# A two-layer hybrid decoder on one core: the final norm goes into the loop over halves of the last tiles, and the hooked parts get new places

## The chip, the cores and the metric

One core of a Trainium2 chip runs the whole program in one launch. The metric is device time in microseconds (us), as the median of several runs; the profile shows one execution of the program. Times in this document are counted from the start of the profiled span.

## The reference

The input x is 512 tokens of 1024 numbers, mem is 256 tokens of 1024, all in 32-bit floats. Two layers follow each other, then a final RMS norm:

```
for l in range(DEPTH):
    xn = rmsnorm(h, norm_mix_g[l])
    c_q, c_kv, k_r, u = split(xn @ w_in[l])
    a_out = mla_group(c_q, c_kv, k_r, ...)        # causal attention, 8 heads, low-rank q and kv, rope
    s_out = s5_group(u, lam, log_dt, b, c, d, w_glu, b_glu)   # 32 groups, 64 complex states, scan, gelu, gate
    h = h + concat(rmsnorm(a_out, ga), rmsnorm(s_out, gs)) @ w_out[l]
    h = h + memory_cross_attention(rmsnorm(h, gx), rmsnorm(mem, gm), w_xq, w_xkv, w_xo)
    h = h + (silu(rmsnorm(h, gf) @ w_gate[l]) * (rmsnorm(h, gf) @ w_up[l])) @ w_down[l]
return rmsnorm(h, final_norm_g)
```

rmsnorm(x, g) is x / sqrt(mean(x^2) + 1e-6) * g over the 1024 (or 512) numbers of a token.

## The kernel before, in words

Everything is held transposed: h is eight tiles (hs[0] to hs[7]) of 128 features by 512 tokens. Each weight block is loaded into a tile wraw and split into a high part whi (ScalarE, ACT, L213) and a low part wlo (VectorE, DVE, L214), and activations likewise into hi and lo (with the gain of a norm: ghi and glo, L245 and L246). A product is then three matmuls of TensorE (PE): high by high, low by high, high by low (mm3, L220 to L222). mm, f, s and t are PSUM tiles; s5b, tmp, tmps, P are buffers in SBUF that several steps share; raw holds matrices that are read from HBM as they are.

A norm (rms) squares and sums the tiles (ACT L264, DVE L267), sums over features with matmuls against ones (L298), makes the statistic on DVE (L301), its power of -1/2 on GpSimd (POOL, L303), and spreads it to a row R over all partitions: ACT makes the high part (L280), DVE the low part (L281), PE multiplies both with the identity (L285), ACT copies the result to R (L306).

Within a layer the order of the code is: input projection (u, c_kv, k_r, c_q), memory norm (memg, its splits are at L245 and L246), the latent attention in units u of one head and query block each, the mix norm of both groups' outputs and w_out (L996 to L998, L1010 to L1012), cross attention, feed-forward. The state-space group and the cross attention's keys and values are cut into parts that are called at units of the attention by the table PLAN: p are steps of the state-space parameters (L374 to L573), v the s-matmuls on u (L820), c the two halves of the scan (L838 to L847, L867), m and y the output (L882, L885), G the gelu (L902), g the gate (the matmuls into t, L918, L919), x the cross attention's keys and values (xv: L961 to L963), s the state-space half of the mix norm. FPLAN does the same for layer 1's parameter steps at tiles of layer 0's feed-forward. The scheduler issues what is ready by a running priority; OFFS, P_OFF, PR_UP and MS_UP shift that priority for a part, so that a part can be issued earlier or later than where it is called. A simulated timeline decides the final order on each engine.

MST_POOL, POOLQ and IN_POOL choose what POOL does in DVE's place: the memory's square sums (L394, seven of 128x256), a share of layer 1's parameter products (L573, L509; twelve of 128x512), the low parts of some input-projection weights (L214).

The last feed-forward chunk of layer 1 leaves its last two output tiles (TAIL = 2) for the end and computes them by halves of 256 tokens. final() then squares and scales the tiles, makes the norm of each half and multiplies the eight tiles of the half by R (L1149): half 1 all on DVE, half 2 with tiles 2 and 6 on POOL. Two tiles go out with each store on the DMA queue of SyncE (SP).

Of the kernel before, what the change touches and what calls it, by code (L numbers as in the profile page):

```python
# [13 lines left out]
AF = mybir.ActivationFunctionType  # L14
ALU = mybir.AluOpType
# [10 lines left out]
EPS = 1e-6  # L26
# [3 lines left out]
KT = DM // 128  # L30
# [18 lines left out]
HALVES = (slice(0, 256), slice(256, 512))  # L49
# [89 lines left out]
class Trunk:  # L139
    def __init__(self, ctx, tc, A, out, depth=L, dbg=None):  # L140
        self.tc, self.nc, self.A, self.out, self.dbg = tc, tc.nc, A, out, dbg or {}
        self.sb = ctx.enter_context(tc.tile_pool(name="sb", bufs=1))
        self.ps = ctx.enter_context(tc.tile_pool(name="ps", bufs=1, space=PSUM))
        self.dr = ctx.enter_context(tc.tile_pool(name="dr", bufs=1, space=DRAM))
        self.depth = depth
        self.stop = self.STOP or depth
        self.n = self.np = 0
# [3 lines left out]


    XKV_POOL = ()
    GLU_POOL, MG_POOL, QK_POOL, ROPE_POOL, MST_POOL = 1, 0, 0, 0, 1
    POOLQ = ((), (1, 3))
    P_OFF = (500, 3000)
    SQ_PARTS, XLO_POOL = (0, 2, 4), ()
    IN_POOL = ((2, 5), (3, 6))
    KE_POOL, GL_POOL = ((0, 2), (0, 2)), ((), ())
    MN_POOL, MW_POOL = ((), ()), ((), ())  # L160
    YT, GT = "f", "t"
# [3 lines left out]


    PLAN = ((
# [5 lines left out]
    ), (  # L173
# [4 lines left out]
    ))  # L178
    OFFS = ({"x": 150, "m": 400, "s": 200, "c": 150, "G": 100, "v": 700, "g": 100, "y": -250, "p": 100},
            {"y": -700, "c": 250, "v": 50, "g": 800, "m": 850, "G": 1300, "p": 100, "x": -100, "s": -50})  # L180
    FPLAN = (0, 0, 1, 1, 1, 1, 1, 1, 2, 5)
    PR_UP, MS_UP = 1500, 2300

    def t(self, shape, tag, dtype=F32, name=None):
        self.n += 1
# [100 lines left out]
                                 start=x is hi, stop=x is lo)  # L286
        return ps

    def rms(self, acc, dim):

        nc = self.nc
        acc = acc if isinstance(acc, list) else [acc]
        n = acc[0].shape[-1]
        nb = n // 128
        ps = self.p("t")
        for b in range(nb):
            for i, x in enumerate(acc):
                nc.tensor.matmul(ps[:, b:b + 1], x[:, b * 128:(b + 1) * 128], self.ones, start=i == 0,  # L298
                                 stop=i == len(acc) - 1)
        ms = self.t([128, 4], "stat")[:, :nb]  # L300
        nc.vector.tensor_scalar(ms, ps[:, :nb], 1.0 / dim, EPS, ALU.mult, ALU.add)  # L301
        col = self.t([128, 4], "stat")[:, :nb]
        nc.gpsimd.tensor_tensor(col, ms, self.mhalf[:, :nb], ALU.pow)  # L303
        ps2 = self.row(col)
        R = self.t([128, 512], "R")[:, :n]
        nc.scalar.activation(R, ps2, AF.Copy)  # L306
        return col, R


# [107 lines left out]
    def s5_gen(self, l):  # L417
# [86 lines left out]
        def cmul_wide(wk, ri, t0, x, y, op, qs):  # L504
            E = V if ri == 0 or (qs.start // 4) not in self.POOLQ[l] else P
            tt = self.t([128, 4, 8, 16], "tmps")
# [5 lines left out]
        for q in range(4):  # L512
# [14 lines left out]
        for q in range(4):  # L527
# [569 lines left out]
    def ffn(self, l, hook):  # L1097
        nc, A = self.nc, self.A
        if l + 1 < self.depth:
            self.dh = self.dram([KT, 128, S], f"dh{l}")  # L1100
        X, R = self.normed(l, "ffn")
        for ci, (k0, nk) in enumerate(FF_CHUNKS):
            Ys = []
            for m in range(k0, k0 + nk):
                pg = self.pm()
                self.mm_block(A["w_gate"][l, m], X, pg)
                gf = self.t([128, 512], "tmp")
                nc.vector.tensor_tensor(gf, pg, R, ALU.mult)  # L1108
                nc.scalar.activation(gf, gf, AF.Silu)
                pu = self.pm()  # L1110
                self.mm_block(A["w_up"][l, m], X, pu)
                uf = self.t([128, 512], "tmp")
                nc.vector.tensor_tensor(uf, pu, R, ALU.mult)  # L1113
                nc.gpsimd.tensor_tensor(uf, uf, gf, ALU.mult)  # L1114
                Ys.append(self.split(uf))
                hook(m)
            last = ci == len(FF_CHUNKS) - 1
            nt = self.TAIL if last and l + 1 == self.depth else 0
            for m in range(KT - nt):
                ps = self.pm()  # L1120
                self.mm_block(A[f"w_down{ci}"][l, m], Ys, ps)
                self.residual(ps, m, self.dh if last and l + 1 < self.depth else None)
                hook(22 + 8 * ci + m)
            if nt:
                ws = [self.load_w_slots(A[f"w_down{ci}"][l, m]) for m in range(KT - nt, KT)]
                for cs in HALVES:
                    for m in range(KT - nt, KT):
                        ps = self.pm()[:, :256]
                        self.mm3(ps, [([w[:, k % 4 * 128:k % 4 * 128 + 128] for w in ws[m - KT + nt][k // 4]],
                                       [y[:, cs] for y in Ys[k]]) for k in range(nk)])  # L1130
                        h = self.hs[m][:, cs]
                        nc.vector.tensor_tensor(h, ps, h, ALU.add)

    def final(self):
        nc = self.nc
        hs = self.hs
        acc = None
        n0 = KT - self.TAIL
        for k in range(n0):
            acc = self.square(acc, hs[k])  # L1140
            nc.scalar.activation(hs[k], hs[k], AF.Copy, scale=self.fin[:, k:k + 1])
        for cs in HALVES:
            for k in range(n0, KT):
                self.square(acc[:, cs], hs[k][:, cs])
                nc.scalar.activation(hs[k][:, cs], hs[k][:, cs], AF.Copy, scale=self.fin[:, k:k + 1])
            _, R = self.rms(acc[:, cs], DM)
            for k in range(KT):
                h = hs[k][:, cs]
                (nc.gpsimd if cs.start and k % 4 == 2 else nc.vector).tensor_tensor(h, h, R, ALU.mult)  # L1149
                if k % 2 == 1:  # L1150
                    nc.sync.dma_start(self.out[k - 1:k + 1, :, cs].rearrange("k p t -> p k t"),
                                      self.hb[k // 4][:, k % 4 - 1:k % 4 + 1, cs])

    def part(self, f, i, off):
        with self.later(off):
# [2 lines left out]
    def run(self):  # L1158
        with self.later(-3 * self.PR_UP):
            self.setup()  # L1160
        for l in range(self.stop):
            self.l = l
            with (self.later(-2 * self.PR_UP) if l == 0 else nullcontext()):
                X, R, du = self.in_proj(l)
            if l == 0:
# [4 lines left out]
                for u, f, i in self.PLAN[0]:  # L1170
                    if u == -4:
                        self.part(params, i, self.OFFS[0].get("p", 0))
            with (self.later(-self.PR_UP) if l == 0 else nullcontext()):
                self.load_u(du)
                if l == 0:
                    for u, f, i in self.PLAN[0]:
                        if u == -3:
                            self.part(params, i, self.OFFS[0].get("p", 0))
                self.in_proj2(l, X, R)
# [5 lines left out]
            for u, f, i in self.PLAN[l]:  # L1185
                if u < -2:
                    continue
                hooks.setdefault(u, []).append((self.part, (parts[f], i, self.OFFS[l].get(f, 0))))
            for f, a in hooks.get(-2, ()):
# [8 lines left out]
            def hook(u):  # L1198
                for i, x in enumerate(self.FPLAN if params else ()):
                    if x == u:  # L1200
                        self.part(params, i, 0)
            self.ffn(l, hook)
        self.final()


@with_exitstack
# [16 lines left out]
```

## Time and profile before

| what | value |
|---|---|
| median of three runs | 1598.01 us (1595.21 to 1603.22) |
| the profiled execution | 1595.71 us |
| its span | 1593.9 us |
| mean granted clock of PE | 0.97 |
| PE busy | 1519.3 us, 95% |
| DVE, ACT, POOL busy | 908.6, 627.0, 169.7 us |
| DMA | 173 MB, mean 109 GB/s |

The span is the time from the first to the last event of the profiled execution. PE's clock is given as a share of 2.4 GHz; 1.2 GHz is 0.50. A timeline row gives the start, the busy time, the engine, the line, the operation, what it writes and reads, and how often it stands there in a row; in brackets how long the engine was idle before and what ended that. The waits list sums such idle times by what ended them. The windows add up each engine's busy time in a stretch.

### The profile page before, as it was taken

How to read it: one execution, taken by the hardware profiler on the slowest of the kernel's cores; microseconds unless marked ns; L12 is line 12 of the kernel's file. 1: busy time of each engine (PE TensorE's matmuls, PEld its weight loads, DVE VectorE, ACT ScalarE, POOL GpSimd, SP SyncE). 2: the span in 40 equal slices, each digit the busy share in tenths (PEclk: the TensorE clock that was granted, in tenths of full speed). 3: DMA queues.
4: the chain of work that ended last, by engine and by line, in shares of the span. 5: the costliest groups of instructions: out<-in, count | busy, mean ns of one | idle time of the engine just before them, and what ended most of it. 6: DMA issues, size and time to landing. Idle time of an engine off the chain costs nothing.

```text
span 1593.9 us, 20203 instructions
## 1 busy us (share of the span) xinstructions
PE 1519.3 (95%) x8038; PEld 1258.6 (79%) x8038; DVE 908.6 (57%) x1274; ACT 627.0 (39%) x1027; POOL 169.7 (11%) x123
## 2 busy tenths in 40 slices
PE   7977999999999999999999899999999999999997
PEld 6766877887877888888886788778887888888886
DVE  7997546657685535435444954465655443543554
ACT  5543475444342322223333456644434222222333
POOL 4300001111131101101100100101000100110110
PEclk9987998999999999999999899999999999999998
DMA  6646633211352332232338454422122223223231
GB/s 222 156 139 152 131 121 119 94 67 53 126 146 93 112 106 93 87 112 93 109 132 158 127 143 124 138 74 93 40 79 94 79 93 106 93 87 112 93 92 62
DMA packets 93278, 173.27 MB, mean 109 GB/s; under 512 B 16512, under 2 KB 49792, under 8 KB 93184
## 3 DMA queue, kind: packets, MB, share of 16 engines
q1 hardware_dynamic: 93184, 171.99, 36.3%
q8 instruction: 63, 1.03, 0.3%
q14 instruction: 31, 0.25, 0.1%
HBM read 152.10 MB, written 17.76 MB: 107 GB/s over the span
## 4 chain that ended last, share of the span: by engine, by line
PE 83%; DVE 6%; DMA 4%; ACT 4%; issue 1%; SPq 1%; POOL 0%; DVEq 0%; ACTq 0%; POOLq 0%
PE mm L220 14%; PE mm L222 13%; PE mm L221 13%; PE f L220 7%; PE f L222 7%; PE f L221 7%; PE mm L768 2%; DVE lo L243 1%; PE t L760 1%; DVE wlo L214 1%; DMA s5b<-dQ 1%; ACT whi L213 1%; PE f L961 1%; PE f L962 1%; PE f L963 1%
## 5 line engine op out<-in xcount | busy, mean ns | idle before, releaser
L213 ACT ACTIVATE whi<-wraw 128x1024 fp32r<-128x1024 f32 (+1 forms) x234 | 243.6, 1043 | 643.8 <-PE mm L221 290.4
L214 DVE TENSOR_TENSOR wlo<-wraw,whi 128x1024 fp32r<-128x1024 f32 (+1 forms) x227 | 312.6, 1378 | 99.0 <-ACT whi L213 96.5
L220 PE MATMUL mm<-hi,whi 128*128 128x512 f32 x580 | 227.3, 392 | 0.5 <-ACT whi L213 0.5
L221 PE MATMUL mm<-lo,whi 128*128 128x512 f32 x580 | 225.8, 390 | 0.0
L222 PE MATMUL mm<-hi,wlo 128*128 128x512 f32 x580 | 225.7, 390 | 0.0
L220 PE MATMUL mm<-ghi,whi 128*128 128x512 f32 (+1 forms) x352 | 138.3, 393 | 1.6 <-DVE tmp L1108 0.8
L222 PE MATMUL mm<-ghi,wlo 128*128 128x512 f32 (+1 forms) x352 | 138.7, 394 | 0.0
L221 PE MATMUL mm<-glo,whi 128*128 128x512 f32 (+1 forms) x352 | 137.8, 391 | 0.2 <-DVE glo L243 0.2
L220 PEld LDWEIGHTS mm<-hi,whi 128*128 128x128 f32 x580 | 109.0, 188 | 26.0 <-ACT whi L213 2.8
L222 PEld LDWEIGHTS mm<-hi,wlo 128*128 128x128 f32 x580 | 108.8, 188 | 23.3 <-DVE wlo L214 0.4
L221 PEld LDWEIGHTS mm<-lo,whi 128*128 128x128 f32 x580 | 108.9, 188 | 22.4
L1114 POOL TENSOR_TENSOR tmp<-tmp,tmp 128x512 f32<-128x512 f32 x44 | 62.2, 1413 | 567.2 <-DVE tmp L1113 520.1
L220 PE MATMUL f<-ghi,whi 128*128 128x512 f32 (+1 forms) x304 | 107.0, 352 | 8.1 <-DVE s5b L950 2.4
L220 PE MATMUL f<-hi,whi 128*128 128x512 f32 x286 | 112.7, 394 | 1.6 <-DVE glo L243 1.4
L222 PE MATMUL f<-hi,wlo 128*128 128x512 f32 x286 | 111.9, 391 | 0.4 <-DVE wlo L214 0.4
L221 PE MATMUL f<-lo,whi 128*128 128x512 f32 x286 | 111.8, 391 | 0.0
L221 PE MATMUL f<-glo,whi 128*128 128x512 f32 (+1 forms) x304 | 106.6, 351 | 0.2 <-DVE glo L243 0.2
L222 PE MATMUL f<-ghi,wlo 128*128 128x512 f32 (+1 forms) x304 | 106.5, 350 | 0.3 <-DVE wlo L214 0.3
L969 DVE TENSOR_TENSOR s5b<-mm,s5b 128x512 f32<-128x512 f32 x53 | 36.6, 691 | 115.9 <-PE mm L222 96.7
L242 ACT ACTIVATE hi<-tmp 128x512 fp32r<-128x512 f32 (+1 forms) x100 | 62.5, 629 | 91.7 <-POOL tmp L1114 63.8
L220 PEld LDWEIGHTS mm<-ghi,whi 128*128 128x128 f32 (+1 forms) x352 | 66.0, 187 | 16.5 <-DVE tmp L1108 1.0
L222 PEld LDWEIGHTS mm<-ghi,wlo 128*128 128x128 f32 (+1 forms) x352 | 66.1, 188 | 14.8 <-DVE tmp L1108 0.3
(330 smaller groups left out, 2821.8 us busy)
## 6 DMA issues: line engine op xcount, KB each, us to landing
wraw<-w_gate SPq DMA_DIRECT2D x44, 512.0 KB, 3.3
wraw<-w_up SPq DMA_DIRECT2D x44, 512.0 KB, 3.3
wraw<-w_down SPq DMA_DIRECT2D x30, 448.0 KB, 3.3
wraw<-w_xkv SPq DMA_DIRECT2D x16, 512.0 KB, 4.0
wraw<-w_xv SPq DMA_DIRECT2D x16, 512.0 KB, 3.5
wraw<-w_out SPq DMA_DIRECT2D x16, 512.0 KB, 3.3
wraw<-w_xq SPq DMA_DIRECT2D x16, 512.0 KB, 3.3
wraw<-w_xo SPq DMA_DIRECT2D x16, 512.0 KB, 3.3
```

The source lines that it names most:

```text
L213: nc.scalar.activation(hi, raw, AF.Copy)
L214: (eng or nc.vector).tensor_tensor(lo, raw, hi.bitcast(F32), ALU.subtract)
L220: self.nc.tensor.matmul(ps, wh, xh, start=i == 0, stop=False)
L221: self.nc.tensor.matmul(ps, wh, xl, start=False, stop=False)
L222: last = self.nc.tensor.matmul(ps, wl, xh, start=False, stop=i == n - 1)
L242: a = nc.scalar.activation(hi, src, AF.Copy)
L243: b = eng.tensor_tensor(lo, src, hi.bitcast(F32), ALU.subtract)
L760: nc.tensor.transpose(pt[:, x * 128:(x + 1) * 128], p[ii][:, kb * 128:(kb + 1) * 128], self.ident)
L768: nc.tensor.matmul(po[64 * x:64 * x + 64, cs], vs[kb][:, (2 * pair + x) * 64:(2 * pair + x + 1) * 64], PT[x][:, kk * 256:min(n, kk * 256 + ...
L961: nc.tensor.matmul(o, xh[:, ts], wh[:, ks], start=hf == tb == k == 0, stop=False)
L969: self.nc.vector.tensor_tensor(self.hs[m], ps, self.hs[m], ALU.add)
L1114: nc.gpsimd.tensor_tensor(uf, uf, gf, ALU.mult)
```

## The change

The final norm is no longer a function behind the feed-forward but three that the loop over halves calls: tail_start squares and scales the six finished tiles, tail_end does the rest for each half as soon as its two tiles are done, tail_scale multiplies by the row. The row is made by two matmuls of plain 32-bit floats from POOL's power (L1163), with no split. Half 1's eight products are ordered behind half 2's statistic. Half 2's products read the row from PSUM on DVE (five) and from its copy on POOL (tiles 2, 4, 6).

PLAN, OFFS, P_OFF, FPLAN, PR_UP and MS_UP get new numbers, and the work that MST_POOL, POOLQ and IN_POOL gave to POOL goes to DVE (seven square sums, twelve parameter products; one low part of 128x512 in layer 0, two of 128x1024 in layer 1). R_UP = 0 shifts nothing, and PSB gives the PSUM tiles as many buffers as before. In the changed file the lines behind the table are 3 and more higher: L220 is L223, L285 is L288, L298 is L301, L820 is L829, L961 is L970.

```diff
-    GLU_POOL, MG_POOL, QK_POOL, ROPE_POOL, MST_POOL = 1, 0, 0, 0, 1
-    POOLQ = ((), (1, 3))
-    P_OFF = (500, 3000)
+    GLU_POOL, MG_POOL, QK_POOL, ROPE_POOL, MST_POOL = 1, 0, 0, 0, 0
+    POOLQ = ((), ())
+    P_OFF = (2850, 4550)
-    IN_POOL = ((2, 5), (3, 6))
+    IN_POOL = ((1, 3), ())
-        (2, "m", 1), (2, "x", 3), (3, "m", 2), (3, "m", 3), (3, "x", 4), (4, "c", 0), (4, "c", 1), (8, "y", 0),
-        (10, "y", 1), (11, "y", 2), (11, "y", 3), (13, "G", 0), (13, "g", 0), (14, "x", 5), (14, "g", 1),
-        (14, "x", 6), (14, "g", 2), (15, "g", 3), (16, "x", 7), (16, "s", 0),
+        (2, "m", 1), (2, "x", 3), (2, "m", 2), (3, "m", 3), (3, "c", 0), (3, "x", 4), (4, "c", 1), (5, "y", 0),
+        (9, "y", 1), (10, "y", 2), (10, "y", 3), (13, "G", 0), (13, "g", 0), (14, "g", 1), (14, "g", 2),
+        (15, "x", 5), (15, "x", 6), (15, "g", 3), (15, "x", 7), (16, "s", 0),
...
-    OFFS = ({"x": 150, "m": 400, "s": 200, "c": 150, "G": 100, "v": 700, "g": 100, "y": -250, "p": 100},
-            {"y": -700, "c": 250, "v": 50, "g": 800, "m": 850, "G": 1300, "p": 100, "x": -100, "s": -50})
-    FPLAN = (0, 0, 1, 1, 1, 1, 1, 1, 2, 5)
-    PR_UP, MS_UP = 1500, 2300
+    OFFS = ({"x": 250, "m": 450, "s": -150, "c": 300, "G": -500, "v": 600, "g": -150, "y": -150, "p": 450},
+            {"y": -1300, "c": -300, "g": 250, "m": 1800, "G": 1550, "x": -100, "s": -300})
+    FPLAN = (2, 5, 6, 6, 13, 17, 19, 23, 29, 33)
+    PR_UP, MS_UP = 2000, 1400
...
+    def tail_end(self, cs):
+
+        nc, hs = self.nc, self.hs
+        for k in range(KT - self.TAIL, KT):
+            self.square(self.acc[:, cs], hs[k][:, cs])
+            nc.scalar.activation(hs[k][:, cs], hs[k][:, cs], AF.Copy, scale=self.fin[:, k:k + 1])
+        col = self.rms_col([self.acc[:, cs]], DM)
+        if cs.start:
+            self.tail_scale(HALVES[0], self.tail_R, self.stat_ins)
+        ps = self.p("t")[:, :256]
+        for b in range(2):
+            nc.tensor.matmul(ps[:, b * 128:(b + 1) * 128], col[:, b:b + 1].to_broadcast([128, 128]), self.ident,
+                             start=True, stop=True)
+        R = self.t([128, 512], "R")[:, :256]
+        nc.scalar.activation(R, ps, AF.Copy)
+        self.tail_R = (R, R)
+        if cs.start:
+            self.tail_scale(cs, (ps, R))
+
+    def tail_scale(self, cs, Rs, dep=None):
+        nc, hs = self.nc, self.hs
+        for k in range(KT):
+            h = hs[k][:, cs]
+            if k in (2, 4, 6) and cs.start:
+                nc.gpsimd.tensor_tensor(h, h, Rs[1], ALU.mult)
+            else:
+                self.after(nc.vector.tensor_tensor(h, h, Rs[0], ALU.mult), dep)
```

The rows of an engine's order below name the line, the operation, its output and inputs (128x512 is the output's shape, x4 that four stand in a row).

PE where layer 1's input projection passes from k_r to w_cq (whi and wlo of w_cq's first block are the last two inputs), before:

```order
L220 MATMUL mm_6967<-ghi_6644,whi_6969 128x512
L221 MATMUL mm_6967<-glo_6645,whi_6969 128x512
L298 MATMUL t_6901<-ones_109,tmp_6899 128x1 x4
L820 MATMUL s_7076<-s5b_6857,raw_7078 64x64
L222 MATMUL mm_6967<-ghi_6644,wlo_6968 128x512
L220 MATMUL mm_6967<-ghi_6650,whi_6969 128x512
```

and now, first the same place, then what stands behind w_cq's first 24 matmuls (the s-matmul's line is L829 now):

```order
L223 MATMUL mm_6967<-ghi_6644,whi_6969 128x512
L224 MATMUL mm_6967<-glo_6645,whi_6969 128x512
L301 MATMUL t_6901<-ones_109,tmp_6899 128x1 x4
L225 MATMUL mm_6967<-ghi_6644,wlo_6968 128x512
```

```order
L224 MATMUL mm_6967<-lo_6693,whi_6969 128x512
L225 MATMUL mm_6967<-hi_6692,wlo_6968 128x512
L223 MATMUL mm_7004<-ghi_6644,whi_7006 128x512
L224 MATMUL mm_7004<-glo_6645,whi_7006 128x512
L829 MATMUL s_7096<-s5b_6857,raw_7098 64x64
L225 MATMUL mm_7004<-ghi_6644,wlo_7005 128x512
```

The first s-matmul on u stood straight behind the statistic's matmuls (L298); now it stands behind all matmuls of w_cq's first block and two of its second.

PE at the mix norm of layer 0 (t_2555 is the state-space group's statistic, t_2610 the attention's, t_2568 the first's row), before:

```order
L768 MATMUL mm_2216<-lo_2452,hi_825 64x128
L768 MATMUL mm_2216<-lo_2458,hi_825 64x128
L298 MATMUL t_2555<-ones_109,tmp_2544 128x1 x4
L285 MATMUL t_2568<-identr_115,cs_2564 128x128
L298 MATMUL t_2610<-ones_109,tmp_2599 128x1 x4
L285 MATMUL t_2568<-identr_115,cs_2565 128x128
```

and now, at the first statistic and at the second:

```order
L970 MATMUL f_2351<-whi_2353,ghi_755 128x256
L971 MATMUL f_2351<-wlo_2352,ghi_755 128x256
L972 MATMUL f_2351<-whi_2353,glo_756 128x256
L301 MATMUL t_2555<-ones_109,tmp_2544 128x1 x4
L777 MATMUL mm_2216<-lo_2521,hi_819 64x256
L777 MATMUL mm_2216<-lo_2515,hi_825 64x128
L777 MATMUL mm_2216<-lo_2521,hi_825 64x128
L970 MATMUL f_2351<-whi_2353,ghi_763 128x256
```

```order
L288 MATMUL t_2568<-identr_115,cs_2564 128x128
L288 MATMUL t_2568<-identr_115,cs_2565 128x128
L301 MATMUL t_2610<-ones_109,tmp_2599 128x1 x4
L970 MATMUL f_2430<-whi_2432,ghi_755 128x256
L971 MATMUL f_2430<-wlo_2431,ghi_755 128x256
L972 MATMUL f_2430<-whi_2432,glo_756 128x256
```

Both statistics and both rows followed each other with nothing between; now matmuls of xv (L970 to L972) stand between each statistic and its row.

DVE at the end of the program (R_12614 and R_12562 are half 1's rows, R_12652 and t_12637 half 2's), before:

```order
L281 TENSOR_TENSOR cs_12606<-stat_12603,cs_12605 128x2
L301 TENSOR_SCALAR stat_12639<-t_12636 128x2
L1149 TENSOR_TENSOR s5b_8654<-s5b_8654,R_12614 128x256 x4
L1149 TENSOR_TENSOR s5b_8656<-s5b_8656,R_12614 128x256 x4
L281 TENSOR_TENSOR cs_12644<-stat_12641,cs_12643 128x2
L1149 TENSOR_TENSOR s5b_8654<-s5b_8654,R_12652 128x256 x3
L1149 TENSOR_TENSOR s5b_8656<-s5b_8656,R_12652 128x256 x3
```

and now:

```order
L270 TENSOR_TENSOR tmp_12451<-tmp_12451,tmp_12614 128x256
L304 TENSOR_SCALAR stat_12621<-t_12618 128x2
L1178 TENSOR_TENSOR s5b_8654<-s5b_8654,R_12562 128x256 x4
L1178 TENSOR_TENSOR s5b_8656<-s5b_8656,R_12562 128x256 x4
L1178 TENSOR_TENSOR s5b_8654<-s5b_8654,t_12637 128x256 x3
L1178 TENSOR_TENSOR s5b_8656<-s5b_8656,t_12637 128x256 x2
```

The low part of half 2's row (L281) that stood behind half 1's products is gone, and half 2's products on DVE are five instead of six, with a PSUM tile as input.

## Rows read from the trace of the kernel before

**Rows 1.** The page's part 1: busy us (share of the span) and instructions of each engine.
```profile
PE 1519.3 (95%) x8038; PEld 1258.6 (79%) x8038; DVE 908.6 (57%) x1274; ACT 627.0 (39%) x1027; POOL 169.7 (11%) x123
```

**Rows 2.** Waits of PE: who waited, for what; us in total, times, longest.
```profile
PE mm L220 <- DVE tmp L720: 6.2, 2, 5.1
...
PE s L820 <- DMA s5b<-du: 3.0, 1, 3.0
```

**Rows 3.** Windows: stretch, busy us by engine, granted PE clock, DMA share, GB/s.
```profile
10.00:60.00 50.00, 49.04 (x234) 39.06 (x234) 45.41 (x96) 24.04 (x43) 27.61 (x17) 1.00 0.64 183
80.00:150.00 70.00, 52.16 (x494) 44.70 (x494) 63.95 (x101) 27.40 (x56) 0.15 (x1) 0.84 0.67 165
261.00:284.00 23.00, 19.97 (x79) 15.93 (x77) 13.66 (x33) 7.45 (x14) 6.40 (x5) 0.70 0.15 50
395.00:475.00 80.00, 78.62 (x451) 63.24 (x451) 58.95 (x81) 31.04 (x47) 22.05 (x14) 0.99 0.43 130
876.00:896.00 20.00, 17.27 (x135) 14.15 (x132) 16.91 (x28) 10.39 (x19) 1.70 (x2) 0.66 0.51 171
```

**Rows 4.** Timeline of DVE in the tail: start, us, operation, idle before.
```profile
1581.77 0.16 DVE L301 TENSOR_SCALAR stat<-t 128x2 f32<-128x2 f32 x1 [0.82 <-PE t L298]
1582.93 2.77 DVE L1149 TENSOR_TENSOR s5b<-s5b,R 128x256 f32<-128x256 f32 x8 [1.00 <-ACT R L306]
...
1587.18 3.15 DVE L1149 TENSOR_TENSOR s5b<-s5b,R 128x256 f32<-128x256 f32 x6 [1.41 <-ACT R L306]
```

**Rows 5.** Timeline of POOL in the tail.
```profile
1582.01 0.70 POOL L303 TENSOR_TENSOR stat<-stat,mhalf 128x2 f32<-128x2 f32 x1 [1.49 <-DVE stat L301]
1587.23 1.82 POOL L1149 TENSOR_TENSOR s5b<-s5b,R 128x256 f32<-128x256 f32 x2 [4.52 <-ACT R L306]
```

**Rows 6.** Timeline of PE where layer 1's input projection ends.
```profile
855.54 0.95 PE L298 MATMUL t<-ones,tmp 128*128 128x1 f32 x8
859.48 0.30 PE L820 MATMUL s<-s5b,raw 128*64 128x64 f32 x2 [2.99 <-DMA s5b<-du]
...
861.38 0.63 PE L222 MATMUL mm<-ghi,wlo 128*128 128x512 f32 x1
...
864.37 0.40 PE L220 MATMUL mm<-hi,whi 128*128 128x512 f32 x1
...
866.46 0.39 PE L220 MATMUL mm<-ghi,whi 128*128 128x512 f32 x1
```

**Rows 7.** Timeline of PE around layer 0's mix norm.
```profile
264.13 0.48 PE L285 MATMUL t<-identr,cs 128*128 128x128 f32 x1 [1.82 <-ACT cs L280]
...
271.87 0.80 PE L997 MATMUL f<-lo,whi 128*128 128x512 f32 x1 [0.71 <-DVE lo L243]
...
275.12 0.79 PE L997 MATMUL f<-lo,whi 128*128 128x512 f32 x1 [0.32 <-DVE lo L243]
```

**Rows 8.** Timeline of PE, the last y matmuls of layer 0.
```profile
211.66 1.10 PE L882 MATMUL f<-s5b,raw 128*128 128x64 f32 x8
```

**Rows 9.** Timeline of DVE, the low parts of layer 0's second gelu half.
```profile
229.00 1.28 DVE L243 TENSOR_TENSOR lo<-tmps,hi 128x512 fp32r<-128x512 f32 x2
```

**Rows 10.** Timeline of DVE in layer 0's opening.
```profile
24.05 1.21 DVE L378 SCALAR_TENSOR_TENSOR P<-P,P 128x512 f32<-128x512 f32 x1
25.18 0.72 DVE L376 SCALAR_TENSOR_TENSOR s5b<-s5b 128x48 f32<-128x48 f32 x1
...
33.09 0.16 DVE L281 TENSOR_TENSOR cs<-stat,cs 128x4 fp32r<-128x4 f32 x1 [3.23 <-ACT cs L280]
```

**Rows 11.** Timeline of POOL in layer 0's opening.
```profile
23.66 4.61 POOL L394 TENSOR_TENSOR tmps<-tmps,tmps 128x256 f32<-128x256 f32 x4
```

**Rows 12.** Timeline of DVE, one small operation alone.
```profile
285.01 0.21 DVE L376 SCALAR_TENSOR_TENSOR s5b<-s5b 128x48 f32<-128x48 f32 x1
```

**Rows 13.** Line L573 by shape: min, median, max ns, first and last start.
```profile
L573 POOL TENSOR_TENSOR s5b<-s5b x2: 1804/2008/2211, 393.7 to 412.2; 128x512 f32<-128x512 f32 x2
```

**Rows 14.** Line L246 by shape, columns as in the group before.
```profile
L246 DVE SCALAR_TENSOR_TENSOR glo<-tmps,gn,ghi x16: 477/482/489, 94.2 to 874.4; 128x256 fp32r<-128x256 f32 x16
```

More of the change, by code (lines that the diff above doesn't have):

```diff
@@ L141, in __init__ @@
         self.tc, self.nc, self.A, self.out, self.dbg = tc, tc.nc, A, out, dbg or {}
+        self.BUFS = dict(self.BUFS, **dict(zip(("mm", "f", "s", "t"), self.PSB)))
         self.sb = ctx.enter_context(tc.tile_pool(name="sb", bufs=1))
@@ L167 @@
     PLAN = ((
[5 rows of a table removed]
-    ), (
[4 rows of a table removed]
-    ))
-    OFFS = ({"x": 150, "m": 400, "s": 200, "c": 150, "G": 100, "v": 700, "g": 100, "y": -250, "p": 100},
-            {"y": -700, "c": 250, "v": 50, "g": 800, "m": 850, "G": 1300, "p": 100, "x": -100, "s": -50})
-    FPLAN = (0, 0, 1, 1, 1, 1, 1, 1, 2, 5)
-    PR_UP, MS_UP = 1500, 2300
[5 rows of a table added]
+    ), (
[4 rows of a table added]
+    ))
+    OFFS = ({"x": 250, "m": 450, "s": -150, "c": 300, "G": -500, "v": 600, "g": -150, "y": -150, "p": 450},
+            {"y": -1300, "c": -300, "g": 250, "m": 1800, "G": 1550, "x": -100, "s": -300})
+    R_UP = 0
+    PSB = (2, 1, 3, 2)
+    FPLAN = (2, 5, 6, 6, 13, 17, 19, 23, 29, 33)
+    PR_UP, MS_UP = 2000, 1400
     def t(self, shape, tag, dtype=F32, name=None):
@@ L287, in row, with rms_col @@
         return ps
-    def rms(self, acc, dim):
+    def rms_col(self, acc, dim):
         nc = self.nc
@@ L300, in rms @@
         ms = self.t([128, 4], "stat")[:, :nb]
-        nc.vector.tensor_scalar(ms, ps[:, :nb], 1.0 / dim, EPS, ALU.mult, ALU.add)
+        self.stat_ins = nc.vector.tensor_scalar(ms, ps[:, :nb], 1.0 / dim, EPS, ALU.mult, ALU.add)
         col = self.t([128, 4], "stat")[:, :nb]
         nc.gpsimd.tensor_tensor(col, ms, self.mhalf[:, :nb], ALU.pow)
-        ps2 = self.row(col)
-        R = self.t([128, 512], "R")[:, :n]
-        nc.scalar.activation(R, ps2, AF.Copy)
+        return col
+    def rms(self, acc, dim):
+        with self.later(-self.R_UP):
+            col = self.rms_col(acc, dim)
+            ps = self.row(col)
+            R = self.t([128, 512], "R")[:, :ps.shape[-1]]
+            self.nc.scalar.activation(R, ps, AF.Copy)
         return col, R
@@ L1124, in ffn @@
             if nt:
+                self.tail_start()
                 ws = [self.load_w_slots(A[f"w_down{ci}"][l, m]) for m in range(KT - nt, KT)]
@@ L1132, in ffn @@
                         nc.vector.tensor_tensor(h, ps, h, ALU.add)
[L1134 to L1152, printed above, removed]
+                    self.tail_end(cs)
@@ new lines, in tail_start @@
+    def tail_start(self):
+        self.acc = None
+        for k in range(KT - self.TAIL):
+            self.acc = self.square(self.acc, self.hs[k])
+            self.nc.scalar.activation(self.hs[k], self.hs[k], AF.Copy, scale=self.fin[:, k:k + 1])
+    def tail_end(self, cs):
[15 more added lines that the diff above has]
+            self.tail_scale(cs, (ps, R))
@@ new lines, in tail_scale @@
+    def tail_scale(self, cs, Rs, dep=None):
[6 more added lines that the diff above has]
+                self.after(nc.vector.tensor_tensor(h, h, Rs[0], ALU.mult), dep)
+            if k % 2 == 1:
+                nc.sync.dma_start(self.out[k - 1:k + 1, :, cs].rearrange("k p t -> p k t"),
+                                  self.hb[k // 4][:, k % 4 - 1:k % 4 + 1, cs])
@@ L1202, in run @@
             self.ffn(l, hook)
-        self.final()
 @with_exitstack
```

12 rows, old and new, of the table PLAN are left out of this document.

## The prediction

> **What bounds the kernel now.** I read the engines' shares first, then what TensorE (PE) waits for, then the windows, then the timeline at the three places where its order changes. PE is busy 95% of the span, VectorE (DVE) 57% [rows 1], so the program is one long queue of matmuls and only its holes can be won: waits of PE, stretches in which PE runs at the lower clock, and the ends of the span. The waits are few: 5.1 us for one rope product (L720) and 3.0 us for layer 1's u [rows 2]. The windows show where the rest lies [rows 3]: layer 0 at 80 to 150 us has PE busy for 52.16 of 70 us at a mean granted clock of 0.84, layer 0's mix norm at 261 to 284 has 0.70, layer 1's start at 876 to 896 has 0.66. With levels of 2.4 and 1.2 GHz, 0.70 over 23 us is 13.8 us at the low one. In the same rows DVE is busy for 45.41 of 50 us at 10 to 60, 63.95 of 70 and 16.91 of 20: DVE bounds the openings, so what the change hands to DVE matters there, and hardly at 395 to 475 (58.95 of 80).
>
> The sum is made against the profiled execution, 1595.7 us; the median of the three runs, 1598.0, lies 2.3 above it. About 0.5%, 8 us, is what a measurement can tell from no change: faster means below 1590.0, slower above 1606.0.
>
> **Tail.** Before, half 2's statistic stands at 1581.77, DVE then takes half 1's eight scales (2.77 us, 0.35 each), only then the low part of half 2's row, and the last six scales run from 1587.18 to 1590.33 [rows 4]; the span ends 3.57 later. After, the statistic does not wait for half 1's row matmuls, so I put it at 1581.4. Eight scales end at 1584.2. Meanwhile POOL's power (0.70 [rows 5]), two plain matmuls and a copy make the row; I put it ready at 1584.0, since the four split matmuls and copy of before needed about 1.3 us from the low part to the scales. Five DVE scales of 0.35 to 0.53 each (alone, and beside POOL: 3.15 over 6) end between 1586.0 and 1586.8; three on POOL of 0.91 each (1.82 for two [rows 5]) at 1586.7. So the last is over near 1586.8 instead of 1590.3: **-3.5**, bounds -2.5 and -4.4.
>
> **Layer 1's u.** Before, one s-matmul (L820) stands in PE's queue straight behind the norm's statistics and waits 2.99 us for u; after that wait the clock falls, and from 861.38 to 864.37 seven steps take 2.99 us where nine later ones take 2.09 [rows 6]: 0.43 instead of 0.23 each, 1.4 lost. Now that matmul stands 24 matmuls of w_cq later. They need 24 x 0.23 = 5.5 us, more than the wait, and u was there at 859.5. What they need from DVE, w_cq's low part, came from POOL and is now DVE's. **-4.4**; the other bound is 0, if the second matrix of the same matmuls (raw, three buffers) comes late instead.
>
> **Layer 1's memory norm and scan.** Eight low parts (L246) of 0.48 us [rows 14] move from 868 to 876 into the stretch where DVE is busy for 16.91 of 20 us, in exchange for half of the second scan half, which moves behind. Bounds: +3.9 (all eight late) and -4 (the scan's share ahead of the rope products is gone). They oppose each other on one queue and I find no row that favours one: **0**.
>
> **Layer 0's mix norm.** Before, PE waits 1.82 us for the first row, then 0.71 and 0.32 for low parts [rows 7], 2.85 in all, and of the 13.8 us at the low clock some 10.9 are work, half of it lost: 5.5. After, blocks of xv stand between the statistic and the row for both norms, 33 matmuls of 256 columns in the second case, some 0.12 us each by half a 512-column step, 4.0 us, against the 1.82 us that PE stood still for the row. So up to -8.5 is won. But these blocks came from elsewhere: they had stood between y's last matmuls, over at 212.8 [rows 8], and the gate's second half, which could start when its low parts came at 229.6 [rows 9]. Ninety-seven rows of PE's order with 26,752 columns stood there, now 51 with 15,232. The first filled 16.8 us; by the columns, with the plain-precision ones at four times, the second fill about 12.4. If the chain keeps its length, a wait of some 4 us opens, with 1.4 of low clock behind it as at u: +5.4. Together **-3**, bounds -8.5 (the chain shortens) and +2 (the wait is as long as 5.1, with more low clock).
>
> **Layer 0's opening.** Seven square sums (128 x 256, 0.35 each as in the tail) and one low part of 128 x 512 (0.7, twice that) come to DVE: +3.1. But while POOL made four of the sums in 4.61 us [rows 11], DVE's own operations were longer: L378 took 1.21, and L376 on 48 columns 0.72 [rows 10], where the same one takes 0.21 alone [rows 12]. Four of that stretch are 0.5 longer each, which gives about 2.1 back. The remaining 1.0 falls into the idle 3.23 us before 33.09 [rows 10]. What is won is the new spread of the s-matmuls and of layer 0's parameter parts in 80 to 150, where 17.8 us of PE are idle. I take **-2**; bounds -6 (a third of that hole) and +4 (the 3.1 come through to the 5.1 us wait [rows 2], with 0.9 of low clock).
>
> The Trainium skill, SBUF — State Buffer, "SBUF: two separate sides", says that a DVE operation with two SBUF inputs and a GpSimd operation hold a shared port pair by an exclusive lock, so that one blocks for the whole of the other. Here the longer DVE rows beside L394 agree. By that rule the move to DVE is nearly free, and the term stands at -2; without it, it would be near 0 and the sum 1585.
>
> **Layer 1's parameter parts.** The title moves them to feed-forward tiles 2 to 33, but their transposes and stores stand in PE's and SP's order where they stood. What is left are twelve operations from POOL (2.0 us each [rows 13]) to DVE, 0.7 each, 8.3 us into 21 us of idle at 395 to 475 [rows 3]: **+0.5**, bounds 0 and +2.
>
> **Sum.** -3.5 - 4.4 + 0 - 3 - 2 + 0.5 = -12.4, from 1595.7: **1583**.
>
> **Rivals.**
> - *The wait only moves from the mix norm to the gate, and the opening gives nothing.* For it speaks the gelu chain that had no slack [rows 8, 9]. -3.5 - 4.4 + 0.5 = -7.4: 1588.
> - *The plan does not do what it says*: u's wait is replaced by one for the next loads, the rest stays as it was, and only the tail pays. -3.5 + 0.5: 1593. Against it: the order of PE did change.
> - *DVE's queue takes it on the path* (slower). Place: layer 1 at 876 to 896, 3.1 us of idle. Eight low parts (3.9) and two low parts of weights that POOL made (1.4 each, four times 0.35) are more than that. If the rope products are late by all of it, a stretch of low clock as long as the mix norm's (13.8, 6.9 lost) follows: +13.6; with the opening at +4 and the gate at +2, against the -7.9 of tail and u, and +0.5: +12, 1608. It decides from the point where DVE has no idle left before L720. The Trainium skill, Perfetto Trace Analysis, "Optimizing Scalar/DVE Operations", says the same by rule: where DVE is saturated, work may rather be given to GPSIMD; its next sentence, that the two share a port, takes half of that back.
> - *Everything pays*: mix norm -8.5, opening -6, scan -2: -24, 1572.
>
> **Chances.** Forecast 0.50 (its own range 1575 to 1590), gate 0.18, tail only 0.12, DVE 0.10, everything 0.10. The range 1573 to 1598 leaves out the slower rival and part of the last. Faster: 0.47 of the forecast, 0.11 of the gate, 0.10: 0.68. Slower: 0.06. The rest, 0.26, cannot be told from no change.
>
> **What would show it.** No wait for u and full clock at w_cq; last scale 3.6 us before the end, with no DVE operation between half 1's and half 2's scales; window of the mix norm at clock 1.00 with a new wait at the gate for ACT's hi; DVE's operations at 20 to 30 us at their plain length. A wait for L246's or L720's results with clock below 0.66 at layer 1's start would make it wrong.

## The result and the profile after

The changed kernel takes 1576.7 us (median of four runs, 1575.7 to 1584.6), the kernel before 1597.5 (four runs). The ratio is 0.988, 95% interval 0.986 to 0.990. The forecast was 1583 with a range of 1573 to 1598, so it held, but the gain, 20.9 us, is larger than the 12.4 of the sum. The profiled execution took 1577.5 us with a span of 1575.4, 18.5 below the span before.

PE's waits in the changed kernel (engine, line, what it waited for; us in total, times, longest):

```profile
PE s L530 <- DVE s5b L518: 8.2, 4, 3.8
...
PE f L876 <- DMA s5b<-dQ: 4.0, 1, 4.0
PE s L829 <- DMA raw<-dBT: 3.5, 4, 1.9
...
PE t L223 <- ACT hi L245: 2.0, 1, 2.0
```

The wait for u is gone, and that for L720's rope product [rows 2] (L729 now) is down to 0.5 us in all. New is L530, the transposes of layer 0's parameters (L521 before, where PE waited 0.3 us at most), which now wait for DVE; the last row is the gate.

The windows that answer to [rows 3], at the places to which the work has moved, and one more at the gate (220 to 232):

```profile
10.00:60.00 50.00, 49.37 (x239) 40.20 (x238) 43.79 (x103) 23.63 (x41) 15.37 (x9) 1.00 0.67 189
80.00:150.00 70.00, 55.44 (x516) 47.35 (x517) 60.36 (x97) 30.99 (x63) 1.12 (x2) 0.87 0.59 165
220.00:232.00 12.00, 8.38 (x31) 5.78 (x30) 3.90 (x6) 8.42 (x14) 0.00 (x0) 0.86 0.13 48
254.00:277.00 23.00, 22.25 (x141) 19.52 (x139) 18.87 (x42) 12.58 (x22) 8.19 (x4) 1.00 0.35 116
395.00:475.00 80.00, 77.76 (x443) 62.46 (x442) 62.34 (x90) 31.60 (x47) 4.06 (x3) 1.00 0.44 135
865.00:885.00 20.00, 18.17 (x137) 15.13 (x136) 17.14 (x28) 12.23 (x23) 2.20 (x2) 0.66 0.62 196
```

The mix norm (254 to 277) is at full clock, 1.00 for 0.70. DVE is busy for 43.79 us at 10 to 60, less than the 45.41 of before, although it has seven square sums and a low part more. POOL fell from 22.05 to 4.06 at 395 to 475 and DVE rose by 3.4. Layer 1's start has the same clock as before, 0.66.

Where the time went shows when the same matmuls start in both traces (first or last of a line, start in us). Of y and of the transposes the start of the last group is taken:

| mark | before | after | gained since the mark above |
|---|---|---|---|
| last y matmul of layer 0 (L882, L891) | 211.7 | 205.4 | 6.2 |
| first cross scores of layer 0 (L1036, L1045) | 342.6 | 335.6 | 0.8 |
| last transposes of layer 1's parameters (L544, L553) | 513.9 | 507.4 | -0.6 |
| last matmul of k_r's row in layer 1 (L652, L661) | 869.5 | 858.8 | 4.2 |
| last w_out matmul of layer 1, first half (L996, L1005) | 1087.9 | 1071.8 | 5.4 |
| last down matmul (L222, L225) | 1578.9 | 1563.3 | -0.4 |
| end of the span | 1593.9 | 1575.4 | 2.9 |

This compares one execution with one. The runs below left more traces in which PE's order up to a mark is that of before (tail_only, but for the end) or that of the change, and they show how far one trace can be trusted. The same stretches, in us:

| stretch | order of before (two traces) | order of the change: range, mean (traces) | gained by the means |
|---|---|---|---|
| start to the last y matmul | 211.7, 208.8 | 205.4 to 210.3, 208.0 (9) | 2.2 |
| to the first cross scores | 131.0, 132.6 | 128.4 to 130.3, 129.6 (8) | 2.2 |
| to the last transposes | 171.3, 171.5 | 170.2 to 171.9, 171.5 (9) | -0.1 |
| to k_r's row | 355.5, 356.9 | 351.3 (7, all alike) | 4.9 |
| to w_out of layer 1 | 218.4, 218.4 | 212.1 to 215.5, 213.6 (5) | 4.8 |

So the 6.2 us of the first mark are mostly scatter: the profile of the change is the earliest of nine there. (With two traces of the old order the 2.2 itself is rough.) In all of them PE waits at L876 (L867 before) close to 150 us, in the change for a load (4.0 to 7.9 us, ending at 147.6 to 149.9), in the two with the order of before as long, ending at 150.0 and 147.9. Up to there the new order has won nothing that can be seen. In the list of waits of before it is this row:

```profile
PE f L867 <- issue: 5.3, 1, 5.3
```

### The profile page after: what moved, and what is told of

Same layout as the page of the kernel before. It is cut to its first block, busy times and chain, and to the rows that moved or that the text cites. A ratio compares the mean times of both kernels' runs of the same rounds, so it can differ in the third digit from the quotient of the medians.

```text
span 1575.4 us, 20197 instructions
## 1 busy us (share of the span) xinstructions
PE 1508.9 (96%) x8038; PEld 1250.0 (79%) x8038; DVE 910.0 (58%) x1293; ACT 625.1 (40%) x1025; POOL 134.6 (9%) x102
## 4 chain that ended last, share of the span: by engine, by line
PE 83%; DVE 7%; ACT 4%; DMA 3%; issue 2%; POOL 1%; SPq 0%; DVEq 0%; ACTq 0%; POOLq 0%
PE mm L223 14%; PE mm L225 14%; PE mm L224 14%; PE f L223 8%; PE f L225 8%; PE f L224 8%; PE mm L777 2%; DVE lo L246 1%; DVE wlo L217 1%; PE t L769 1%; ACT hi L245 1%; ACT whi L216 1%; PE f L891 1%; PE f L876 1%; PE f L970 1%
## 5 line engine op out<-in xcount | busy, mean ns | idle before, releaser
L217 DVE TENSOR_TENSOR wlo<-wraw,whi 128x1024 fp32r<-128x1024 f32 (+1 forms) x230 | 315.8, 1373 | 95.0 <-ACT whi L216 92.7
L223 PE MATMUL mm<-hi,whi 128*128 128x512 f32 x580 | 226.9, 391 | 0.5 <-ACT whi L216 0.5
L225 PE MATMUL mm<-hi,wlo 128*128 128x512 f32 x580 | 225.5, 390 | 0.0
L223 PE MATMUL mm<-ghi,whi 128*128 128x512 f32 (+1 forms) x352 | 138.0, 392 | 2.8 <-DVE tmp L1117 1.4
L225 PE MATMUL mm<-ghi,wlo 128*128 128x512 f32 (+1 forms) x352 | 138.3, 393 | 0.0
L223 PEld LDWEIGHTS mm<-hi,whi 128*128 128x128 f32 x580 | 108.7, 187 | 25.1 <-ACT whi L216 2.8
L225 PEld LDWEIGHTS mm<-hi,wlo 128*128 128x128 f32 x580 | 108.7, 187 | 23.2 <-DVE wlo L217 0.4
L223 PE MATMUL f<-hi,whi 128*128 128x512 f32 x286 | 112.5, 393 | 1.6 <-DVE glo L246 1.4
L225 PE MATMUL f<-hi,wlo 128*128 128x512 f32 x286 | 112.2, 392 | 0.4 <-DVE wlo L217 0.4
L223 PE MATMUL f<-ghi,whi 128*128 128x512 f32 (+1 forms) x304 | 107.6, 354 | 2.7 <-DVE tmp L1117 1.9
L225 PE MATMUL f<-ghi,wlo 128*128 128x512 f32 (+1 forms) x304 | 107.1, 352 | 0.5 <-DVE wlo L217 0.5
L223 PEld LDWEIGHTS mm<-ghi,whi 128*128 128x128 f32 (+1 forms) x352 | 65.9, 187 | 17.9 <-DVE tmp L1117 1.6
L225 PEld LDWEIGHTS mm<-ghi,wlo 128*128 128x128 f32 (+1 forms) x352 | 65.8, 187 | 15.6 <-issue 1.1
```

The source lines that it names most:

```text
L217: (eng or nc.vector).tensor_tensor(lo, raw, hi.bitcast(F32), ALU.subtract)
L223: self.nc.tensor.matmul(ps, wh, xh, start=i == 0, stop=False)
L225: last = self.nc.tensor.matmul(ps, wl, xh, start=False, stop=i == n - 1)
```

## Experiments

Medians are of the runs of each kernel. Medians of one program scatter by some 2 us: the order of the change was timed twice (1576.7 and, in fplan_old, 1578.5). Where a few us matter I therefore read the marks of the tables too.

**tail_only.** The kernel before with the new tail; in the changed file all tables and choices are set back:

```diff
-    P_OFF = (2850, 4550)
+    P_OFF = (500, 3000)
...
-    PR_UP, MS_UP = 2000, 1400
+    PR_UP, MS_UP = 1500, 2300
```

> The kernel before with the new tail alone (final norm inside the loop over halves), all tables and POOL choices as before. If the parts add up, it is 2.9 us below the kernel before (the last down matmul to the end of the span took 15.0 us before and 12.1 in the change), so about 1594.6, between -2.0 and -4.0. If the new tail only pays together with the rest, it is within 1 us of before.

Measured 1594.2 against 1596.8, ratio 0.9985 (0.9973 to 0.9998): -2.6, as the theory has it. The end of the changed kernel on DVE:

```profile
1565.69 0.16 DVE L304 TENSOR_SCALAR stat<-t 128x2 f32<-128x2 f32 x1 [0.76 <-PE t L301]
1565.76 3.29 DVE L1178 TENSOR_TENSOR s5b<-s5b,R 128x256 f32<-128x256 f32 x8
1568.98 1.73 DVE L1178 TENSOR_TENSOR s5b<-s5b,t 128x256 f32<-128x256 f32 x5
```

Nothing stands between the two groups now. From the start of the last down matmul to the end of the last product it takes 7.4 us where it took 11.4 [rows 4], 4.0 less. But the span ends 4.6 us behind the last product, before 3.6. In the twelve traces with this tail (all but two_first) it takes 11.8 to 12.2 us from that matmul to the end, before 15.0.

**two_first.** Two of half 1's products go ahead of half 2's statistic:

```diff
-                self.after(nc.vector.tensor_tensor(h, h, Rs[0], ALU.mult), dep)
+                self.after(nc.vector.tensor_tensor(h, h, Rs[0], ALU.mult), dep if k > 1 else None)
```

> The change with the first two of half 1's eight final products ahead of half 2's statistic on DVE, so that the first store can be issued some 0.8 us earlier. Theory: the end is bound by the stores (2.1 MB at about 340 GB/s in one piece, 4.7 us from the last product to the end where it was 3.6), so 0.5 to 0.8 us below the change, and the last product no earlier. Rival: the last product bounds the end; then 0 to 0.4 above, since half 2's statistic comes later.

What the DMA engines did in the last 13.9 us of the changed kernel (busy tenths in 40 slices, and GB/s):

```profile
DMA  0000000000000000069999995999999999950000
GB/s 0 0 0 0 0 0 0 0 0 0 0 0 0 0 0 0 0 233 318 360 327 351 351 304 200 330 354 333 354 348 339 321 374 330 345 180 9 0 0 0
```

and in the last 13.9 us of the kernel before:

```profile
DMA  0000000000000499999999300009969999993000
```

The new tail has one block of stores without an idle slice at some 340 GB/s; before, half 1's stores were out before half 2's began. In two_first the first products on DVE stand ahead of the statistic:

```profile
1569.54 0.75 DVE L1178 TENSOR_TENSOR s5b<-s5b,R 128x256 f32<-128x256 f32 x2
1570.39 0.16 DVE L304 TENSOR_SCALAR stat<-t 128x2 f32<-128x2 f32 x1
1570.46 2.09 DVE L1178 TENSOR_TENSOR s5b<-s5b,R 128x256 f32<-128x256 f32 x6
```

From the last down matmul (1568.0) to the end (1579.0) it takes 11.0 us for 12.1. The part is shorter by 1.1, but the last product came earlier too (one on POOL, 6.8 us behind that matmul, instead of one on DVE at 7.4), which I had not expected, so the run does not separate the two explanations. The whole, 1577.1 us, cannot be told from the change.

**fplan_old.** The tables for layer 1's parameter parts (FPLAN and the second number of P_OFF) set back:

```diff
-    P_OFF = (2850, 4550)
+    P_OFF = (2850, 3000)
-    FPLAN = (2, 5, 6, 6, 13, 17, 19, 23, 29, 33)
+    FPLAN = (0, 0, 1, 1, 1, 1, 1, 1, 2, 5)
```

> The change with FPLAN as before and layer 1's P_OFF of before (3000), which is what its title speaks of. Theory: these numbers move no instruction on any engine, so the time is that of the change within the scatter of runs, 1576.7 within 1.5 us. Rival: layer 1's parameter parts do move and give a part of the gain; then 1 to 5 us above.

Measured 1578.5 (1576.0 to 1581.5), ratio to before 0.9886 (0.9867 to 0.9904), for 0.9877 of the change: the same. The order of every engine is that of the change, row for row. The new places of layer 1's parameter parts do nothing.

**wcq_low_pool.** One low part of 128x1024 in layer 1 back on POOL:

```diff
-    IN_POOL = ((1, 3), ())
+    IN_POOL = ((1, 3), (6,))
```

> The change with one weight's low part (w_cq's first block of layer 1) back on POOL. In the order this alone puts the first s-matmul on u back straight behind the statistic. Theory: the 4.9 us gained there hang on that one place, so the wait of about 3 us for u and the low clock behind it return and the time is 4 to 5 us above the change. Rival: they hang on layer 1's plan, or u comes earlier now; then the time is that of the change within 1 us.

Measured 1584.2, ratio 0.9916 (0.9899 to 0.9932): by the ratios some 6 us above the change, 5 above fplan_old, which has the same order. The first s-matmul in its trace, and then the changed kernel's:

```profile
854.50 0.45 PE L829 MATMUL s<-s5b,raw 128*64 128x64 f32 x2 [2.70 <-DMA s5b<-dQ]
```

```profile
855.61 0.33 PE L829 MATMUL s<-s5b,raw 128*64 128x64 f32 x2
```

The wait is back, at the place that it had in [rows 6] (the tile that is named has another label here); from the transposes to k_r's row it takes 356.2 us, in the change 351.3, before 355.5. So layer 1's u is not helped by the plan: a low part that DVE makes itself moved this matmul in PE's order. (Two later pairs of s-matmuls move by a few rows with it.)

**plan1_old, layer1_old, scan_old.** Layer 1's plan and offsets back; the same with both of layer 1's low parts on POOL; the offset of the scan alone back:

```diff
-            {"y": -1300, "c": -300, "g": 250, "m": 1800, "G": 1550, "x": -100, "s": -300})
+            {"y": -700, "c": 250, "v": 50, "g": 800, "m": 850, "G": 1300, "p": 100, "x": -100, "s": -50})
```

```diff
-    IN_POOL = ((1, 3), ())
+    IN_POOL = ((1, 3), (3, 6))
```

```diff
-            {"y": -1300, "c": -300, "g": 250, "m": 1800, "G": 1550, "x": -100, "s": -300})
+            {"y": -1300, "c": 250, "g": 250, "m": 1800, "G": 1550, "x": -100, "s": -300})
```

> The change with layer 1's PLAN and OFFS of before; the first s-matmul keeps its new place. Theory: the 4.7 us between 873 and 957 us come from the scan's parts standing ahead of the memory norm's splits, so the time is 4 to 5.5 above the change, with waits for L720's and L950's results back in layer 1's first units. Rival: they come from work that left POOL and DVE's relief; then at most 1 us above the change.

> The change with layer 1's PLAN and OFFS of before and, besides, layer 1's two low parts of weights back on POOL. From the end of layer 0's parameter transposes to the last matmul of layer 1's mix norm the change took 564.4 us, before 574.0; each of the two edits alone gave back 5.7 and 2.0. Theory: both remove the same later waits (2.4 us for L950's result, 1.5 for L720's), so that they don't add: together 573 to 574.5 in that stretch, 9 to 10 above the change. Rival: they add, 572 and 7 to 8 above; the rest then came from the twelve parameter products that left POOL.

> The change with the offset of layer 1's scan parts as before (250 for -300) and nothing else. Theory: what layer 1's plan gives (2.0 us in its stretch when undone alone) is the earlier scan, so 1 to 3 us above the change. Rival: it is the later memory norm or the output parts; then within 1 us.

Measured 1580.7 (ratio 0.9898, 0.9884 to 0.9913), 1583.5 (0.9923, 0.9900 to 0.9946) and 1587.5 (0.9943, 0.9927 to 0.9960). From the transposes to the end of layer 1's mix norm the profiles have 566.4, 572.7 and 571.7 us; the change 564.4, before 574.0. So plan1_old is within its expectation by the median, 4.0, but not by the stretch, 2.0, and the waits that I had named are not back in it. The stretch is no proof of any loss: with the order of the change it took 563.3 to 566.7 in four other traces, and behind k_r's row plan1_old takes 215.0 us, inside the 212.1 to 215.5 of the change and well below the 218.4 of before. The old plan of layer 1 by itself thus leaves most of the gain there standing. layer1_old is 6 to 7 us above the change, below both expectations; its stretch lies between what they said, so it does not tell whether the two edits add. In neither run is PE's order in layer 1's first units that of before. scan_old is above its own: one number costs more than the whole set to which it belongs. Its waits stand later, most of them at the output parts, and so does its low clock:

```profile
952.93 0.50 PE L223 MATMUL mm<-hi,hi 128*128 128x512 f32 x1 [1.08 <-ACT hi L245]
...
978.89 0.39 PE L970 MATMUL f<-whi,ghi 128*128 128x256 f32 x1 [2.01 <-ACT s5b L974]
```

```profile
950.00:970.00 20.00, 18.91 (x125) 16.08 (x125) 8.19 (x16) 12.90 (x26) 0.00 (x0) 0.83 0.53 157
1030.00:1050.00 20.00, 17.40 (x71) 14.11 (x71) 12.48 (x21) 9.04 (x16) 1.99 (x1) 0.74 0.08 27
```

The change at the output parts, and at its mix norm, which comes some 7 us earlier:

```profile
950.00:970.00 20.00, 20.00 (x157) 17.54 (x156) 9.47 (x18) 15.92 (x35) 0.00 (x0) 1.00 0.48 137
```

```profile
1023.00:1043.00 20.00, 17.20 (x75) 13.77 (x73) 13.71 (x22) 10.25 (x18) 1.99 (x1) 0.83 0.09 27
```

At the mix norm PE is idle for nearly as long in the change; matched matmul by matmul, scan_old falls behind by some 6 us between 950 and 985 and by only 1 more at the mix norm.

These numbers act as a set. An undone one shifts what the scheduler issues from there on, and its price is that of the new order (here a third one, neither that of before nor that of the change), not of the one wait for which it was undone.

**squares_pool.** The seven sums back on POOL:

```diff
-    GLU_POOL, MG_POOL, QK_POOL, ROPE_POOL, MST_POOL = 1, 0, 0, 0, 0
+    GLU_POOL, MG_POOL, QK_POOL, ROPE_POOL, MST_POOL = 1, 0, 0, 0, 1
```

> The change with the memory's seven square sums back on POOL. Theory: POOL's sums lengthen DVE's operations beside them by about as much (2.1 us) as the sums cost on DVE (2.4), so L376 on 48 columns is about 0.7 us long again and the time is that of the change within 1.5 us. Rival: DVE is the bound of the opening and any work on it is on the path; then 2 to 3 us below the change. Other rival: the relief of DVE was what made the opening 5 us shorter; then 2 to 5 above.

Measured 1578.7, ratio 0.9886 (0.9868 to 0.9903): that of fplan_old. DVE beside POOL's sums in this run, and the same operations in the change:

```profile
24.46 1.22 DVE L387 SCALAR_TENSOR_TENSOR P<-P,P 128x512 f32<-128x512 f32 x1
25.60 0.73 DVE L385 SCALAR_TENSOR_TENSOR s5b<-s5b 128x48 f32<-128x48 f32 x1
```

```profile
24.46 0.68 DVE L387 SCALAR_TENSOR_TENSOR P<-P,P 128x512 f32<-128x512 f32 x1
25.06 0.20 DVE L385 SCALAR_TENSOR_TENSOR s5b<-s5b 128x48 f32<-128x48 f32 x1
```

One choice lengthens them from 0.68 to 1.22 and from 0.20 to 0.73 us. Both are 0.53 to 0.54 longer, whatever their size, beside sums of 1.15 us each (4.60 for four). That agrees with the exclusive lock of which the Trainium skill, SBUF — State Buffer, "SBUF: two separate sides", speaks. It also fits that the sums cost the same time on either engine: seven of 0.42 us on DVE, or operations on DVE that wait.

**s_old.** The state-space half of layer 0's mix norm at its old priority:

```diff
-    OFFS = ({"x": 250, "m": 450, "s": -150, "c": 300, "G": -500, "v": 600, "g": -150, "y": -150, "p": 450},
+    OFFS = ({"x": 250, "m": 450, "s": 200, "c": 300, "G": -500, "v": 600, "g": -150, "y": -150, "p": 450},
```

> The change with the state-space half of layer 0's mix norm at its old priority (200 for -150). In the order its statistic and row go back towards the attention's, with a few xv matmuls between the first statistic and the first row matmul, and the second row straight behind. The gate's order is the same. Theory: the waits and the low clock at the mix norm return in part, 3 to 8.5 us above the change. Rival: the blocks that are left between still cover the rows; within 1 us of the change.

Measured 1584.0, ratio 0.9922 (0.9907 to 0.9937), 6 to 7 above the change, inside the theory's interval. From y's last matmuls to the first cross scores it takes 135.0 us, more than the change (128.4 to 130.3) and than before (131.0 and 132.6): undone, the place costs more than it had won. Its mix norm:

```profile
266.87 0.80 PE L1005 MATMUL f<-hi,whi 128*128 128x512 f32 x1 [2.19 <-ACT hi L245]
...
271.45 0.80 PE L1006 MATMUL f<-lo,whi 128*128 128x512 f32 x1 [3.36 <-DVE lo L246]
```

```profile
254.00:277.00 23.00, 17.31 (x105) 15.22 (x104) 15.58 (x26) 11.06 (x19) 3.89 (x3) 0.78 0.33 116
```

PE waits 5.55 us (2.19 and 3.36) for the normed tiles and the clock is 0.78 where the change has 1.00. This is the clearest effect of one number in layer 0.

**plan0_old, plan0_old_squares_pool, plan0_only.** Layer 0's plan, offsets and leads of before; the same with the sums on POOL; plan and offsets of before with the new leads:

```diff
-    P_OFF = (2850, 4550)
+    P_OFF = (500, 4550)
...
-    PR_UP, MS_UP = 2000, 1400
+    PR_UP, MS_UP = 1500, 2300
```

(these lines are not in plan0_only, which keeps the new P_OFF too; PLAN[0] and OFFS[0] are those of before in all three.)

> The change with layer 0's PLAN, OFFS, P_OFF, PR_UP and MS_UP of before. Theory: all of layer 0's gain (7.0 us at the first matmul of its cross attention) is the plan's, so the time is 6 to 8 above the change, with low clock at the mix norm back. Rival: the square sums on DVE (no lengthened DVE operations beside POOL) gave a part of it; then 3 to 5 above.

> Layer 0's plan of before as in the run plan0_old, and the seven square sums back on POOL. Theory: the sums are as cheap on DVE with the old plan as with the new, so the time is that of plan0_old, 1586.9, within 2 us. Rival: plan0_old was slow because the old plan has no room on DVE for them; then 3 to 6 below it.

> The change with layer 0's PLAN and OFFS of before, but the new PR_UP and MS_UP. Theory: the places and offsets carry layer 0's gain, so the time is that of plan0_old, 1586.9, within 2 us. Rival: the larger lead of the first projection and the smaller one of the memory's sums carry half of it; then 1580 to 1584.

Measured 1586.9 (ratio 0.9947), 1586.8 (0.9938) and 1587.6 (0.9942). The sums are as cheap with the old plan as with the new, as the second theory says. The first is 10 above the change, more than 6 to 8: its layer 0 is slower than before. Its waits:

```profile
PE f L876 <- DMA s5b<-dQ: 7.5, 1, 7.5
PE mm L223 <- ACT hi L245: 5.1, 4, 3.7
```

The first of them is no longer than in the traces of the change (4.0 to 7.9 us), but it ends at 154.2 us, and at 158.0 in plan0_old_squares_pool, where there it ends before 150.

The first cross scores of layer 0 start at 350.8, 349.7 and 341.8 us, in the change at 335.6, before at 342.6. So the third agrees with its expectation only in the total: its layer 0 is 8 to 9 faster than that of the other two, and its layer 1, whose order also changed, 5 to 7 slower. So both the places and the leads, or P_OFF with them, matter for layer 0. Why the old plan does worse with the rest of the change than before (350 for 343) stays open. Its order of PE is not that of before either: the two part at 44 us. The sums are not the reason, and the one low part of layer 0 that also went to DVE was not tried alone.

## Why the prediction was right, and where not

- **Tail, -3.5:** measured -2.9 in the profile and -2.6 as a part alone. Right in mechanism; the sum took the 3.57 us behind the last product as fixed, and they became 4.6. That the stores now come in one block would explain it, but two_first does not separate this from the earlier product. The products themselves gained 4.0: half 1's eight took longer than I had put (3.29 for 2.77), half 2's five less, 0.35 each beside POOL.
- **Layer 1's u, -4.4:** -4.2 in the profile, -4.9 by the means of the traces, and 4.9 lost when the one place was undone. Right, and through the step that was named: the low part that is now DVE's.
- **Memory norm and scan, 0:** the mis-sized term. It gave -5.4 in the profile and -4.8 by the means up to the end of layer 1's mix norm, past its bound of -4. I had set eight late low parts against a shorter scan queue and taken the middle. In the trace the added low parts did not make PE late, and its holes behind them shrank, as the same 36 us of layer 1's first units show, of the kernel before:

```profile
896.00:932.00 36.00, 30.70 (x223) 27.89 (x222) 28.68 (x41) 18.76 (x36) 2.66 (x2) 1.00 0.63 132
```

  and 11 us earlier in the change:

```profile
885.00:921.00 36.00, 33.85 (x247) 30.83 (x246) 34.62 (x56) 22.80 (x47) 2.19 (x2) 1.00 0.48 127
```

  DVE is busy for 34.62 of 36 us and PE still waits less, so DVE's load was not what set this stretch. That the order of its work was is likely, but not shown: with the scan's offset of before the stretch from the transposes to the mix norm is 7.3 us longer (scan_old), but the loss lies at other places, plan1_old kept most of the gain, and no edit brought the old order or the old waits back. What closed the holes stays open.
- **Mix norm, -3:** -0.8 in this profile from y's last matmuls on, -2.6 in that of fplan_old, -2.2 by the means. The window is at full clock, as foreseen, and the new wait is at the gate:

```profile
222.06 0.51 PE L223 MATMUL t<-hi,whi 128*128 128x512 f32 x1 [1.97 <-ACT hi L245]
```

  It is 1.97 us where I had 4, with clock 0.86 over 12 us, 1.7 lost where I had 1.4. Undoing the norm's place costs 6 to 7 (s_old). So both halves of the term were there; the wait was half as long, and what was won is smaller than the -8.5, which the term's own parts (2.85 and 5.5) make 8.35.
- **Opening, -2:** -6.2 in the profile, -2.2 by the means of nine traces with this order and two with the old. The size was right, but it was a share taken of the idle hole, and the way was not the one I had in mind: up to the load at about 150 us nothing is won, and the 2 us lie behind it. The relief of DVE is as I read it from the lengthened rows, but it is worth little by itself (squares_pool), and the sums took 0.42 us each where I had 0.35.
- **Layer 1's parameter parts, +0.5:** +0.6 lost in the profile between cross attention and the transposes, +0.1 by the means, which is nothing within the scatter. fplan_old shows that the tables for these parts do nothing; the twelve products were not put back on POOL alone.
- **Sum:** by the means the terms are -2.9, -4.9, -4.8, -2.2, -2.2 and 0.1, together some -17, for -12.4; the medians of the change and of fplan_old lie 18 to 21 below before. Most of what was missing is the one term that I had set at the middle of its bounds for want of a row, memory norm and scan, 0 for -4.8. The opening, which by the one profile looks like 4 us more, is not among it. The slower rival did not occur: low clock at layer 1's start is as before.

## What to carry to other kernels

In a program that is one queue of matmuls, look for the matmul that stands behind a wait in the order while others that could run stand behind it: one such place was worth 5 us here, and what moved it was one low part that went to another engine. A row that is waited for, like a norm's, can be covered by work put between the statistic and its use, and the clock then stayed up as well; but count where that work is missing afterwards (6 to 7 us lost here when it was undone, some 2 won by the whole move). Tuned priorities act as a set: a single one can cost more when undone than the set gives, so its price undone is not its share of the gain. A number that moves no row of the order is worth nothing. And before a few us between two profiles are explained, compare several traces of the same order.

## What the runs showed of the hardware

- GpSimd's sums of 128x256 beside VectorE lengthened a VectorE operation on 48 columns from 0.20 to 0.73 us, and one on 512 from 0.68 to 1.22.
- VectorE's products of 128x256 take 0.35 us each where GpSimd does not hinder them. Six with both inputs in SBUF took 3.15 us [rows 4] while GpSimd made two, that is some 1.1 longer; five with one input in PSUM took 1.73 while GpSimd made three, no longer than without it.
- Five products with a PSUM tile as one input took 1.73 us, 0.35 each, the six of two_first with both inputs in SBUF 2.09, also 0.35 each. The Trainium skill, Perfetto Trace Analysis, "Optimizing Scalar/DVE Operations", gives a larger access overhead for PSUM; in a row of products it does not show here.
- Eight stores of 256 KB from SBUF to HBM in one block went at some 340 GB/s with the DMA engines busy at nine tenths or more in most slices; the 2.1 MB took some 6.6 us (19 slices).
